# A two-layer decoder trunk: products with V followed at once by the next logits, forget-gate sums later in the order

## The chip, the cores and the metric

The kernel runs on one core of one Trainium2 chip. The metric is the device time of one execution in microseconds (us). Lower is better. Five engines matter: TensorE (PE in the rows, PEld its weight loads), VectorE (DVE), ScalarE (ACT), GpSimd (POOL) and SyncE (SP), which here only issues transfers.

## The reference, cut to what matters

x is 256 tokens by 1024 features, in float32. There are two layers, each a mixer of four groups of four heads (head width 64; 96 for MLA's queries and keys) and a SwiGLU. Layer 0 has two groups of forgetting attention (Fox) and two of stick-breaking attention, layer 1 has two of MoBA and two of MLA.

```python
for layer in range(2):
    h = rms_norm(x, norm[layer])
    x = x + mixer(h @ w_in) @ w_out          # 4 groups of 4 heads
    h = rms_norm(x, ffn_norm[layer])
    g, u = split(h @ w_gate_up, 2)
    x = x + (silu(g) * u) @ w_down           # 2816 wide

# Fox: q and k are normed for each head, f is one forget gate for each token and head
log_f = log_sigmoid(f + forget_bias)
c = cumsum(log_f, axis=tokens)
logits[t, s] = q[t] . k[s] / 8 + c[t] - c[s]     # s <= t
out = softmax(logits) @ v
```

## The kernel before

**Products.** Each large product is made of three matmuls in the fp32r format: operands are split into a rounded part and a rest (`whi` and `wlo` for weights, `xh` and `xl` for activations), and `mm3` adds three products. ScalarE makes `whi` from the loaded `raw`, VectorE makes `wlo` as the difference, in pieces of 128x512. Weights stream through four `raw` buffers and three pairs of split buffers. Pieces are split ahead of their use: `W.pos` is told how far TensorE is, and issues the splits due.

**Attention.** Logits, transposes and products with V are fp32 matmuls. A group's work is written as `prep` (norms' scaling has made `qkn` for queries and keys; four transposes each, and copies to `fT`), and then, for each of its two pairs of heads, `scores` (the logits into two PSUM banks, then the first step of the softmax or of the stick-breaking weights on VectorE), `transp` (three transposes a head, copied to `wt` by ScalarE) and `values` (products with V into the bank O, shared by the two pairs). After the second pair `outputs` copies O out. Logits, transposes, copies of `fT` and O share four PSUM banks, called `ps`.

**Order.** Between these steps `heads_loop` puts filler: the projections of the later groups and, at the end, three of the four parts of the output projection. A planner, `Flow`, writes the program's order. Its clock `clk` advances with each matmul that is issued, by an assumed cost (122 ns for 256 columns, 107 ns for a transpose). `fl.at(dt, fn)` puts a function due `dt` ns later, and it is called at the first stop of the filler at which the clock has passed the due time. `fl.pull(ns)` issues filler until its goal has grown by `ns`; a unit of filler is mostly one k-tile of a projection, six matmuls of 256 columns, 730 ns by the clock. `fl.need(flag)` issues filler until a flag is set.

The framework then places each engine's instructions, in an order fixed when the program is built: by priority, which is the place in the program, and by its own estimate of when operands are there. Functions marked `urgent` stand 400 places further ahead. On TensorE, functions marked `pinned` may not come before the last matmul issued ahead of them. `scores` is urgent and not pinned, so it may move ahead of filler that is written before it; `transp` and `values` are both urgent and pinned.

In `heads_loop` one iteration handles one pair of heads: the logits of pair i, then filler, the transposes of pair i-1, after every second pair the preparation of the next group, filler, the products of pair i-1, filler. Here `b` is the filler still planned, divided by the pairs still to come.

**The forget gates.** `first` is called before the projections of group 0's queries and keys. It puts these steps due: `chain` (the logs of the gates, `lf`), `gains`, `sums` (two transposes of `lf`, then the scan `cum` along the tokens on VectorE, and transfers of four rows of it to `cbc` for group 1 through DRAM), `columns` (two transposes of `cum`, copied to `ct` by VectorE) and `over(0)` and `over(1)` (four transposes each, which spread columns of `ct` over the partitions, copied to `cbc` by ScalarE). `masks` of group 0 reads `ct` and `cbc`: heads 0 and 1 what `over(0)` has written, heads 2 and 3 what `over(1)` has written. `masks(0)` and `masks(1)` are issued by `prep`, the other two after the first logits.

Of the kernel before, what the change touches and what calls it, by code (L numbers as in the profile page):

```python
# [281 lines left out]
def trunk_kernel(ctx: ExitStack, tc: tile.TileContext, x, ffn_norm, w_gate_up, w_down, rel_bias,  # L282
# [15 lines left out]
    fl = Flow()  # L298
# [12 lines left out]
    def pinned(fn):  # L311

        def f(*a, **k):
            with tc.issue_after(fl.last):
                return fn(*a, **k)
        return f
# [13 lines left out]
    def freed(*a):  # L330
        for t in a:
            read.add(id(t))

    def ps():
        return psB.tile([P, 512], F32, name=nm("ps"), tag="ps")
# [33 lines left out]
    def tr(o, i, idn):  # L369
        fl.last = pe.transpose(o, i, idn).ins  # L370
        fl.clk += 107
# [245 lines left out]
    def v_rows(V, src, scale):  # L617

        for tok in range(2):
            act.activation(V[:, tok], src[tok], AF.Identity, scale=1.0 if scale is None else scale[:, tok:tok + 1])  # L620
        return V
# [133 lines left out]

    def heads_loop(groups, lead):

        n, tail = 2 * len(groups), 6000
        fl.pull(lead)
        pinned(groups[0].prep)()  # L760
        fl.pull(100)
        for i in range(n + 1):
            b = max(fl.total - tail - fl.used, 0) / (n - i) if i < n else tail
            if i < n:
                if i > 0:
                    g.ready(pr, "e")
                g, pr = groups[i // 2], i % 2
                g.scores(pr)
            fl.pull((0.35 if i < n else 0.6) * b)
            if i > 0:  # L770
                g1, pr1 = groups[(i - 1) // 2], (i - 1) % 2
                g1.ready(pr1, "w")
                for j in range(2):
                    g1.transp(2 * pr1 + j)
            if i < n and pr == 1 and i + 1 < n:
                groups[i // 2 + 1].prep()
            fl.pull((0.35 if i < n else 0.15) * b)
            if i > 0:
                if g1.V is None:
                    fl.need(("V", g1))  # L780
                g1.values(pr1)
                if pr1 == 1:
                    g1.outputs()
            fl.pull((0.35 if i < n else 0.25) * b)


    xn = {}
# [208 lines left out]
    def first():  # L996

        zg, ng, ab, ex, lg, lf = (att.tile([P, 2, 8], F32, name=f"fg{i}", bufs=1) for i in range(6))

        @urgent  # L1000
        def chain():
            for tok in range(2):
                dve.scalar_tensor_tensor(zg[:, tok], fa[tok][:, 256:264], X.rs[:, tok:tok + 1], fb8,
                                         OP.mult, OP.add)
            dve.tensor_scalar(ng, zg, -1.0, 0.0, op0=OP.mult, op1=OP.max)
            dve.scalar_tensor_tensor(ab, ng, 2.0, zg, OP.mult, OP.add)
            act.activation(ex, ab, AF.Exp, scale=-1.0)
            act.activation(lg, ex, AF.Ln, bias=1.0)
            dve.tensor_tensor(lf, ng, lg, OP.add)
            groups[0].V = v_rows(vz[0], [t[:, :256].rearrange("p (h d) -> p h d", d=64) for t in fa], X.rs)  # L1010
            freed(*fa)
            fl.flags.add(("V", groups[0]))

        @pinned
        @urgent
        def sums():
            p_ = ps()
            for tok in range(2):
                tr(p_[:8, tok * P:tok * P + P], lf[:, tok], ident)
            dve.tensor_tensor_scan(cum, p_[:8, :256], mcaus[:8, P:P + 1].to_broadcast([8, 256]), 0.0, OP.add, OP.add)  # L1020
            pool.dma_start(cd, cum[4:8])
            pool.dma_start(cbc[:, 4:8], bass.AP(tensor=cd.tensor, offset=cd.offset, ap=[[0, P], [256, 4], [1, 256]]))

        @pinned
        @urgent
        def over(j):
            p_ = ps()
            for i in range(2):
                for tok in range(2):
                    c = tok * 8 + 2 * j + i  # L1030
                    tr(p_[:, i * 256 + tok * P:i * 256 + tok * P + P], ct[:, c:c + 1].to_broadcast([P, P]), ident)
            act.activation(cbc[:, 2 * j:2 * j + 2], p_.rearrange("p (i n) -> p i n", i=2), AF.Copy)

        @pinned
        @urgent
        def columns():
            p_ = ps()
            for tok in range(2):
                tr(p_[:, tok * 8:tok * 8 + 8], cum[:, tok * P:tok * P + P], ident[:8, :8])
            dve.tensor_copy(ct, p_[:, :16])  # L1040
        fl.at(1500, chain)
        fl.at(11800, sums)
        fl.at(13800, columns)
        fl.at(8000, gains)
        for j in range(2):
            fl.at(14300 + 1000 * j, lambda j=j: over(j))

    class Fox(Softmax):
        def mask(self, h):
# [75 lines left out]
    def fill_group(g):  # L1125
        G = groups[g]
        feat = g >= 2
        if g == 0:
            first()
            yield True  # L1130
        pq, pk = Proj(f"q{g}", X, feat), Proj(f"k{g}", X, feat)
        if feat:
            aq, ak = G.rows(pq, pk)
        else:
            aq, ak = G.normed(pq, pk, X.rs, r2, g_fox)
        yield from pq.kts(0, KT)
        if g == 0:
            dve.scalar_tensor_tensor(r2, X.rs[:, 0:2], 1.0 / 64, X.rs[:, 0:2], OP.mult, OP.mult)
        aq()
        yield from pk.kts(0, KT)  # L1140
        ak()
        if g == 0:
            X.row_bc()
            return
        pv = Proj(f"v{g}", X)
        yield from pv.kts(0, KT)
        G.V = urgent(v_rows)(vz[g % 2], heads_of(pv.a), X.rs)
        freed(pv.a)
        fl.flags.add(("V", G))
# [12 lines left out]
    run(fill_group(0))  # L1162
    fl.start(fill0(), 12 * 5235)
    heads_loop(groups, 2500)
    fl.drain()
    fl.finish()
# [249 lines left out]

    fl.start(fill1(), 6 * 5235 + 2 * 3300)
    heads_loop([moba[0], mla[0], moba[1], mla[1]], 2500)
    fl.drain()
    fl.finish()  # L1420
# [49 lines left out]
```

## Time and profile before

| | |
|---|---|
| time, median of 3 runs | 624.66 us (624.04 to 625.13) |
| time of the profiled execution | 625.75 us |
| its span, first to last instruction | 623.6 us |
| mean granted clock of TensorE | 0.997 |
| TensorE busy | 613.6 us |
| VectorE busy | 425.5 us |
| ScalarE busy | 336.2 us |
| attention of layer 0, by the trace | about 24 to 124 us |
| attention of layer 1, by the trace | about 338 to 432 us |

The span is one profiled execution of the program. The durations in the rows of the trace come from it. TensorE's matmuls are pipelined and the ends that the rows show are modelled, so the distance between starts tells more than the durations. The granted clock is a share of 2.4 GHz: 1.00 is full, 0.50 is 1.2 GHz, and a value between them is a mean over a stretch with both. Nearly every row has line 113 (L113), a helper through which all engines' instructions go, so instructions are told apart by their tiles.

### The profile page before, as it was taken

To read this page: it belongs to the slowest core of one execution; us is meant where nothing else is said; L and a number is where in the kernel's file an instruction comes from. 1 tells how busy PE (TensorE), PEld (TensorE's weight loads), DVE (VectorE), ACT (ScalarE), POOL (GpSimd) and SP (SyncE) were. 2 spreads that over 40 slices of the span, in tenths; PEclk is the share of its full clock that TensorE was granted. 3 is DMA by queue.
4 is the path that set the end of the run, shared out by engine and by line. 5 is a ranking of instruction groups with operands and counts; after the bars stand their busy time and mean duration, and the time that the engine had idled before them with its cause. 6 is when DMAs were issued, how large, how long until landed. Compare 5 with 4: busy or idle time off the path is not lost. (4 is left out here: it accounts for less than half of the span.)

```text
span 623.6 us, 11055 instructions
## 1 busy us (share of the span) xinstructions
PE 613.6 (98%) x4370; PEld 563.7 (90%) x4370; DVE 425.5 (68%) x915; ACT 336.2 (54%) x715; POOL 19.5 (3%) x50
## 2 busy tenths in 40 slices
PE   8989999999999999999999999999999999999997
PEld 7978898789999999988889988868999999998897
DVE  4889786576777677745547797977677767774541
ACT  6846675564444544545447676967544454453430
POOL 7200000010000000000000000000000000000000
PEclk9989999999999999999999999999999999999999
DMA  8963434447654754664558344154466465465500
GB/s 253 335 202 105 167 136 136 136 152 255 211 195 143 225 175 154 218 198 152 182 174 276 127 135 136 34 171 136 133 211 198 137 220 185 143 230 188 189 29 34
DMA packets 84213, 106.19 MB, mean 170 GB/s; under 512 B 3533, under 2 KB 69395, under 8 KB 84033
## 3 DMA queue, kind: packets, MB, share of 16 engines
q1 hardware_dynamic: 82880, 101.49, 50.5%
q0 software_dynamic: 1120, 3.86, 1.9%
q8 instruction: 34, 0.56, 0.4%
q14 instruction: 19, 0.15, 0.1%
q10 hardware_dynamic: 160, 0.14, 0.1%
HBM read 104.41 MB, written 3.17 MB: 173 GB/s over the span
## 5 line engine op out<-in xcount | busy, mean ns | idle before, releaser
L113 DVE TENSOR_TENSOR wlo<-raw,whi 128x512 fp32r<-128x512 f32 (+3 forms) x300 | 241.2, 828 | 84.3 <-ACT whi L113 83.7
L113 ACT ACTIVATE whi<-raw 128x512 fp32r<-128x512 f32 (+3 forms) x300 | 208.8, 739 | 142.6 <-PE acc L113 129.1
L113 PE MATMUL acc<-xh,whi 128*128 128x256 f32 x768 | 218.3, 284 | 0.0
L113 PE MATMUL acc<-xh,wlo 128*128 128x256 f32 x768 | 217.7, 284 | 0.0
L113 PE MATMUL acc<-xl,whi 128*128 128x256 f32 x768 | 217.5, 283 | 0.0
L113 PEld LDWEIGHTS acc<-xh,whi 128*128 128x128 f32 x768 | 147.3, 192 | 1.0 <-issue 1.0
L113 PEld LDWEIGHTS acc<-xh,wlo 128*128 128x128 f32 x768 | 147.3, 192 | 0.5 <-issue 0.5
L113 PEld LDWEIGHTS acc<-xl,whi 128*128 128x128 f32 x768 | 147.4, 192 | 0.0
L113 PE MATMUL acc<-whi,hl 128*128 128x512 f32 (+1 forms) x198 | 73.3, 370 | 0.0
L113 PE MATMUL acc<-whi,hh 128*128 128x512 f32 (+1 forms) x198 | 73.2, 370 | 0.0
L113 PE MATMUL acc<-wlo,hh 128*128 128x512 f32 (+1 forms) x198 | 73.1, 369 | 0.0
L113 PE MATMUL acc<-whi,xh 128*128 128x256 f32 (+2 forms) x240 | 71.1, 297 | 0.0
L113 PE MATMUL acc<-whi,xl 128*128 128x256 f32 (+2 forms) x240 | 70.0, 292 | 0.0
L113 PE MATMUL acc<-wlo,xh 128*128 128x256 f32 (+2 forms) x240 | 69.8, 291 | 0.0
L113 ACT ACTIVATE hh<-t 128x256 fp32r<-128x256 f32 x44 | 18.4, 418 | 69.6 <-DVE t L113 69.6
L113 DVE TENSOR_TENSOR gs<-acc,rbc 128x512 f32<-128x512 f32 x44 | 30.4, 691 | 37.0 <-PE acc L113 36.9
L113 PEld LDWEIGHTS acc<-whi,xh 128*128 128x128 f32 x240 | 46.0, 192 | 1.5 <-issue 1.3
L113 PEld LDWEIGHTS acc<-whi,xl 128*128 128x128 f32 x240 | 46.1, 192 | 0.7 <-issue 0.7
L113 PEld LDWEIGHTS acc<-wlo,xh 128*128 128x128 f32 x240 | 46.1, 192 | 0.6 <-issue 0.3
L113 PEld LDWEIGHTS acc<-whi,hh 128*128 128x128 f32 x198 | 37.3, 188 | 6.7
L113 PEld LDWEIGHTS acc<-whi,hl 128*128 128x128 f32 x198 | 37.2, 188 | 6.7
L113 PEld LDWEIGHTS acc<-wlo,hh 128*128 128x128 f32 x198 | 37.3, 188 | 6.7
(178 smaller groups left out, 626.5 us busy)
## 6 DMA issues: line engine op xcount, KB each, us to landing
raw<-in_ffn_w_gate_up SPq DMA_DIRECT2D x44, 1024.0 KB, 5.3
raw<-in_ffn_w_down SPq DMA_DIRECT2D x20, 1024.0 KB, 5.1
raw<-in_ev_w_in SPq DMA_DIRECT2D x10, 1024.0 KB, 8.0
raw<-in_od_w_in SPq DMA_DIRECT2D x6, 1024.0 KB, 5.5
raw<-in_ev_w_out SPq DMA_DIRECT2D x4, 1024.0 KB, 4.9
raw<-in_od_w_out SPq DMA_DIRECT2D x4, 1024.0 KB, 5.0
brep<-bd POOLq DMA_DIRECT2D x1, 2048.0 KB, 10.1
raw<-in_ffn_w_down SPq DMA_DIRECT2D x4, 512.0 KB, 3.7
```

The costliest lines, as they stand in the source:

```text
L113: r = f(*a, **k)
```

## The change

In `heads_loop` the third pull of an iteration is dropped, except in the last iteration, and the first two pulls grow from 0.35 to 0.5 of b. So in the program's order the products of pair i-1 are followed directly by the logits of pair i+1. In `first`, `columns` is due at 16,300 instead of 13,800, and `over(j)` at 16,800 + 1000 j instead of 14,300 + 1000 j. The matmuls, copies and transfers are the same.

```diff
-            fl.pull((0.35 if i < n else 0.6) * b)
+            fl.pull((0.5 if i < n else 0.6) * b)
             if i > 0:
                 g1, pr1 = groups[(i - 1) // 2], (i - 1) % 2
                 g1.ready(pr1, "w")
@@
             if i < n and pr == 1 and i + 1 < n:
                 groups[i // 2 + 1].prep()
-            fl.pull((0.35 if i < n else 0.15) * b)
+            fl.pull((0.5 if i < n else 0.15) * b)
             if i > 0:
                 if g1.V is None:
                     fl.need(("V", g1))
                 g1.values(pr1)
                 if pr1 == 1:
                     g1.outputs()
-            fl.pull((0.35 if i < n else 0.25) * b)
+            if i == n:
+                fl.pull(0.25 * b)
@@
         fl.at(1500, chain)
         fl.at(11800, sums)
-        fl.at(13800, columns)
+        fl.at(16300, columns)
         fl.at(8000, gains)
         for j in range(2):
-            fl.at(14300 + 1000 * j, lambda j=j: over(j))
+            fl.at(16800 + 1000 * j, lambda j=j: over(j))
```

## Rows read from the trace of the kernel before

**Rows 1.** The page, busy time: us, share of the span, instructions.

```profile
PE 613.6 (98%) x4370; PEld 563.7 (90%) x4370; DVE 425.5 (68%) x915; ACT 336.2 (54%) x715; POOL 19.5 (3%) x50
```

**Rows 2.** Waits of TensorE: us in total, times, longest.

```profile
PE ps L113 <- DVE sm L113: 2.2, 1, 2.2
PE ps L113 <- DMA x<-in_x: 1.1, 1, 1.1
```

**Rows 3.** Timeline of TensorE, 30.5 to 34 us: start, duration, [idle before].

```profile
30.97 0.28 PE L113 MATMUL acc<-whi,xh 128*128 128x256 f32 x1
31.09 0.28 PE L113 MATMUL acc<-wlo,xh 128*128 128x256 f32 x1
33.56 0.38 PE L113 MATMUL ps<-ident,cum 8*128 8x8 f32 x2 [2.19 <-DVE sm L113]
```

**Rows 4.** Timeline, 28 to 42 us: the gates' transposes, and VectorE.

```profile
28.25 0.38 PE L113 MATMUL ps<-ident,fg 128*8 128x128 f32 x2
...
32.83 0.67 DVE L113 TENSOR_TENSOR_SCAN cum<-ps,mcaus 8x256 f32<-8x256 f32 x1
...
34.16 0.17 DVE L113 COPY ct<-ps 128x16 f32<-128x16 f32 x1
...
35.05 0.69 DVE L113 TENSOR_TENSOR wlo<-raw,whi 128x512 fp32r<-128x512 f32 x1
37.33 1.41 DVE L113 SCALAR_TENSOR_TENSOR m<-cbc,ct,mcaus 128x128 f32<-128x128 f32 x4 [1.60 <-ACT cbc L113]
...
41.84 0.69 DVE L113 TENSOR_REDUCE sm<-sqh 128x8 f32<-128x512 f32 x1 [0.51 <-ACT sqh L113]
```

**Rows 5.** Stretches: length, busy us (instructions) by engine, granted clock, DMA share, GB/s.

```profile
31.00:34.00 3.00, 0.81 (x7) 0.59 (x5) 3.00 (x8) 0.68 (x3) 0.20 (x1) 0.89 1.06 303
34.00:37.00 3.00, 3.00 (x16) 3.00 (x16) 1.73 (x7) 0.43 (x2) 0.33 (x1) 0.54 0.76 242
37.00:40.00 3.00, 2.92 (x26) 2.75 (x25) 2.67 (x9) 1.50 (x3) 0.59 (x1) 1.00 0.99 314
```

**Rows 6.** Timeline, 36 to 39 us: copies to `cbc`, four transposes at full clock.

```profile
36.62 1.19 ACT L113 ACTIVATE cbc<-ps 128x512 f32<-128x512 f32 x2 [2.57 <-PE ps L113]
...
38.44 0.60 PE L113 MATMUL ps<-ident,qkn 128*128 128x128 f32 x4
```

**Rows 7.** Stretches of layer 0's attention.

```profile
41.50:57.30 15.80, 14.88 (x126) 13.96 (x124) 15.34 (x61) 13.08 (x39) 0.00 (x0) 1.00 0.06 16
57.30:112.00 54.70, 54.70 (x432) 47.80 (x432) 42.14 (x91) 33.57 (x80) 0.00 (x0) 1.00 0.46 154
```

**Rows 8.** Timeline, 41 to 60 us: first logits, group 1's key, products, logits.

```profile
41.57 1.58 PE L113 MATMUL ps<-fT,fT 64*128 64x128 f32 x16
...
55.99 0.68 DVE L113 TENSOR_TENSOR qkn<-acc,sm 128x512 f32<-128x512 f32 x1
...
56.73 0.66 PE L113 MATMUL ps<-ident,qkn 128*128 128x128 f32 x4 [0.92 <-DVE qkn L113]
...
58.11 0.39 PE L113 MATMUL acc<-xh,wlo 128*128 128x256 f32 x1
...
59.02 0.93 PE L113 MATMUL ps<-fT,fT 64*128 64x128 f32 x8
```

**Rows 9.** Timeline of TensorE, 63 to 83 us: logits (fT, sbT) and products (wt).

```profile
63.35 1.30 PE L113 MATMUL ps<-fT,fT 64*128 64x128 f32 x8
...
67.65 0.87 PE L113 MATMUL ps<-wt,V 128*64 128x256 f32 x8
...
74.33 0.87 PE L113 MATMUL ps<-wt,V 128*64 128x256 f32 x8
75.13 0.93 PE L113 MATMUL ps<-sbT,sbT 64*128 64x128 f32 x8
...
81.14 1.65 PE L113 MATMUL ps<-sbT,sbT 64*128 64x128 f32 x8
```

## The prediction

> **What bounds the kernel now.** I read the page first: TensorE is busy for 613.6 of 623.6 us, VectorE for 425.5 [rows 1]. So the span is TensorE's own work plus the little that it loses, and a change of order can win only what is lost: idle time, slow clock, and breaks between kinds of matmul. The list of waits, cut to TensorE, says where: one wait of 2.2 us on VectorE is the largest, every other is 1.1 us or less [rows 2]. The timeline puts it before the two transposes of `columns`: the matmul before them starts at 31.09, they start at 33.56 [rows 3]. They wait for `cum`, the scan of the forget gates' logs. Its input was transposed at 28.25, yet VectorE starts the scan at 32.83 and ends it at 33.50 [rows 4], because VectorE works in order and is full: in 31 to 34 us it is busy for 3.00 of 3.00 [rows 5], with splits of weights (`wlo`) between the steps of two chains. The stretches show a second price: the granted clock is 0.89 in 31 to 34 us, 0.54 in 34 to 37 and 1.00 after that [rows 5]. TensorE's clock has the levels 1.2 and 2.4 GHz, so these mean some 0.66 and 2.76 us at the lower one. In the first stretch TensorE idled through part of that (only from 33.56 on, 0.44 us, does it work), so the loss is (0.44 + 2.76)/2 = 1.6 us. Stall and clock are 2.19 + 1.6 = 3.8 us, the most that the place can give.
>
> **The change: the forget gates.** Nothing is added or removed, only due times move. By the planner's clock, `heads_loop` begins at 12,001 ns (2 x 8 k-tiles of 730 ns and three transposes of 107). `sums` fires after k-tile 1 of the next projection (at 12,731, to 12,945 with its transposes). k-tiles 2 and 3 end at 13,675 and 14,405: there `columns` fires now, due at 13,800. Due at 16,300 it fires after k-tile 6, at 16,595. Three more k-tiles, 18 matmuls at the 0.12 us of rows 3, go ahead of it: 2.16 us of work for a gap of 2.19. TensorE would come to the transposes at about 33.4, when the scan ends. The stall goes almost wholly, and as TensorE then works through, I take the drop of the clock to go too.
>
> What is late next is VectorE. `ct`, the copy behind `columns`, ran at 34.16 between two splits [rows 4]. Three k-tiles later in the order, the splits behind it, the last one at 35.05, may well stand ahead of it, for they are ready and VectorE's order is fixed. So it runs at 34.2 as now or at about 35.75, when the last of them ends. Behind it wait the four transposes of `over(0)`, which fire right after `columns` (16,809 against a due time of 16,800), the copy to `cbc` and the masks. With one k-tile of filler between, TensorE comes to `over(0)` at 34.6 and waits up to 1.3 us. Four transposes take 0.60 us with their drain, half a copy of `cbc` 0.60 [rows 6]; from `ct` at 35.75 to 35.92, with 0.1 for the hand-over, the masks start at 37.2. The other half, `over(1)`, falls behind the first logits; its heads' masks are needed only a pair later.
>
> VectorE is then the limit up to the preparation of group 1. Between 31 and 57.3 us it idles little beyond 1.60 (masks at 37.33, waiting for `cbc`) and 0.51 (a reduce at 41.84) [rows 4, 7]. The scaling of group 1's key, `qkn` at 55.99, stands at the end of that queue, and TensorE's transposes of it at 56.73 already wait 0.92 us for it [rows 8]. However early TensorE comes, it can't pass this point sooner than VectorE lets it. VectorE's gain has two ends. With `ct` late: the masks start 0.13 sooner, the scaling of group 0's key (0.68, as the one at 55.99) moves into the gap before them, and the 0.51 goes, since that reduce waits for a projection which TensorE ends sooner: 1.3 us. With `ct` as early as now, both idle times go: 2.1. I take the middle, 1.7. TensorE's own gain is 3.8 less about 0.7 of new waiting at `over(0)`; what exceeds 1.7, some 1.4, becomes more waiting at 56.73 (0.92 grows to about 2.3). From 57.3 to 112 us TensorE is busy all the time, with VectorE at 42.1 of 54.7 [rows 7], so what is won by then stays won. The ends for the whole place are 0 (all comes back as waiting and slow clock) and 3.8.
>
> The page "TensorE: Matmul & The Clock Gate" of the Trainium skill (its section on the 32x32 sub-arrays) says that ScalarE's and VectorE's queues are strictly first in, first out, and rows 4 agree: the scan waited 4 us behind other work with its input there. By it group 1's key can't overtake the splits and the sum for this place is 1.7; could each step run as soon as its input is there, it would be 3.8.
>
> **The change: the loop.** Dropping the third pull puts each pair's logits behind the products with V in program order, but `urgent` already lets them pass filler. Of the twelve places in both layers where a pair's products are followed by new logits, the logits stand at once behind the products in four (74.33 and 75.13 is one), ahead of the products, behind transposes, in six (63.35, with the products only at 67.65), and only in two is there filler between [rows 8, 9]. In one of these six matmuls fill 58.11 to 59.02, 0.91 us for 6 x 0.12 = 0.72 of work [rows 8]; the other, near 386, has two matmuls. Closing such a break gives back 0.2, so 0.4 for both. Filler that leaves this place goes between transposes and products (0.5 of b instead of 0.35), where the copy of `wt` has more time, which I count as nothing. The filler is the same work: 3 x 0.35 = 1.05 of b becomes 2 x 0.5, and the rest is drained behind. So 0.4, with the ends 0 and 0.4 x 12/2 = 2.4, if every place had such a break.
>
> **Sum.** 1.7 + 0.4 = 2.1 us. The profiled execution took 625.75, 2.15 around its span; with the change its span would be 621.5 and its time 623.65. It lies 1.09 above the median of the runs, 624.66, so I forecast 622.5. A change under 0.2%, 1.25 us, can't be told from none.
>
> **Rivals.**
> - *The whole 3.8 comes through.* VectorE's order is made anew; if the critical steps get ahead of splits, neither `ct` nor the group's key is late. For it: splits run far ahead of their use, so nothing needs them at once. Against it: the same priorities made the order that shows the lag. 3.8 + 0.4 = 4.2, 620.5.
> - *The stall moves and the clock falls again.* TensorE waits up to 1.3 at `over(0)` and 2.3 at group 1's key. In the trace 2.19 us idle was followed by the lower level, 0.92 was not [rows 3, 5, 7, 8]. Another 1.6 lost leaves 0.5: 624.1, the same as before. It decides from a single wait about as long as the old one; against it, the waiting may be spread over `over(0)`, the key of group 0 and both transposes of group 1.
> - *Slower: logits wait for PSUM banks.* With O held, two banks under transposes and no filler between, logits would wait for a bank. Those behind transposes show it: eight records take 1.30 us at 63.35 and 1.65 at 81.14, those behind products 0.93 [rows 9], so 0.37 and 0.72 more. If the other six places came to stand so, at 0.72 each, 4.3 is lost: 624.66 - 2.1 + 4.3 = 626.9. It decides from 0.56 a place, (2.1 + 1.25)/6. Against it: logits right behind products show no such wait now, as `wt` has left its banks by then.
> - *The loop's change does nothing.* The logits' places stay as they are; 1.7 alone, 623.0, still faster.
>
> **Chances.** Forecast, with the last rival: 0.55, own range 621.4 to 623.4. Whole gain: 0.15. Clock falls again, or VectorE keeps nearly all: 0.2. Slower: 0.1. Faster by over 0.2% takes the first two and loses a little at the edge: 0.67; within 0.22; slower 0.11. The range runs from the whole gain, a little below it, 620.2, to a little above the repeated drop, 624.8; it leaves out the slower case and the tails.
>
> **What would show it.** Right: no wait before the transposes of `cum`, granted clock 1.00 over 31 to 37 us; `ct` between 34 and 36; first logits at 39 to 40 instead of 41.57; a longer wait before group 1's key, now near 55; logits in the loops at their old places. Wrong: group 1's key transposed at 53 (whole gain); a second stretch at the lower level in 36 to 58; or logits in the loops that take over 1.3 us each.

## The result

The change made the kernel slower: median 633.63 us (632.83 to 633.89, 4 runs) against 624.89 (624.04 to 625.7, 4 runs), a ratio of 1.0138 [1.012, 1.0155]. The forecast was 622.5 (620.2 to 624.8). The profiled execution took 632.83 us, its span 630.7 at a granted clock of 0.999. The busy line of its page answers [rows 1]:

```profile
PE 622.2 (99%) x4370; PEld 565.5 (90%) x4370; DVE 426.3 (68%) x915; ACT 336.9 (53%) x715; POOL 20.2 (3%) x50
```

As many matmuls as before, yet TensorE is busy for 8.6 us longer, while VectorE and ScalarE are busy as long as before (within 0.8 us). TensorE doesn't wait more for others; its own work takes longer. Its waits (us in total, times, longest), beside [rows 2]:

```profile
PE ps L113 <- DVE sm L113: 1.7, 1, 1.7
...
PE ps L113 <- DVE qkn L113: 0.6, 1, 0.6
PE ps L113 <- DVE ct L113: 0.4, 1, 0.4
```

The stretches (length, busy us and instructions of TensorE, its weight loads, VectorE, ScalarE and GpSimd, granted clock, DMA share, GB/s) say where it happens; they answer [rows 5, 7]:

```profile
31.00:34.00 3.00, 1.28 (x10) 0.91 (x8) 3.00 (x9) 0.42 (x2) 0.53 (x1) 1.00 1.02 289
34.00:37.00 3.00, 2.64 (x22) 2.44 (x22) 2.93 (x11) 1.21 (x3) 0.00 (x0) 1.00 0.73 202
...
41.50:57.30 15.80, 15.24 (x119) 13.56 (x117) 15.01 (x55) 9.90 (x28) 0.00 (x0) 1.00 0.11 28
57.30:112.00 54.70, 54.70 (x400) 46.15 (x399) 37.79 (x83) 31.56 (x75) 0.00 (x0) 1.00 0.43 147
```

At the gates the place is better: clock 1.00, more matmuls by 37 us. From 57.3 to 112 us TensorE is busy all the time, as before, but issues 400 matmuls instead of 432. That is where the loss shows, and a busy share can't show it. TensorE's timeline at such a place (start, duration, shape, count; an fp32 matmul leaves two records, so x2 is one matmul):

```profile
75.20 0.65 PE L113 MATMUL ps<-wt,V 128*64 128x256 f32 x2
75.78 0.48 PE L113 MATMUL ps<-sbT,sbT 64*128 64x128 f32 x2
76.19 0.65 PE L113 MATMUL ps<-wt,V 128*64 128x256 f32 x2
76.77 0.70 PE L113 MATMUL ps<-sbT,sbT 64*128 64x128 f32 x4
77.40 0.43 PE L113 MATMUL ps<-wt,V 128*64 128x128 f32 x2
77.77 0.70 PE L113 MATMUL ps<-sbT,sbT 64*128 64x256 f32 x2
78.39 0.43 PE L113 MATMUL ps<-wt,V 128*64 128x128 f32 x2
78.75 0.38 PE L113 MATMUL acc<-whi,xh 128*128 128x256 f32 x1
```

The four products of a pair (V below) and the four logits of the next (S) are no longer two blocks, VVVVSSSS as at 74.33 and 75.13 of [rows 9], but alternate: VSVSSVSV. From 75.20 to 78.75 they take 3.55 us; as blocks the products took 0.80 (74.33 to 75.13) and the logits 0.85, so 1.65 (the filler behind them starts at 75.98). The place costs 1.90 us more. The trace has four of them (54.80, 75.20, 100.60 and 389.45) and a fifth, VSVSVSVS, in the MLA heads (413.32 to 417.20, 3.88 us against some 2.2 as blocks): 4 x 1.90 + 1.7 = 9.3 us. A part of why an alternating place is dear is seen in its weight loads, which elsewhere overlap the matmuls (in brackets, the idle time ahead of them):

```profile
75.78 0.29 PEld L113 LDWEIGHTS ps<-sbT,sbT 64*128 64x128 f32 x2 [0.38 <-issue]
76.19 0.19 PEld L113 LDWEIGHTS ps<-wt,V 128*64 128x64 f32 x2
76.77 0.30 PEld L113 LDWEIGHTS ps<-sbT,sbT 64*128 64x128 f32 x4 [0.39 <-issue]
77.40 0.19 PEld L113 LDWEIGHTS ps<-wt,V 128*64 128x64 f32 x2 [0.33 <-issue]
77.76 0.29 PEld L113 LDWEIGHTS ps<-sbT,sbT 64*128 64x128 f32 x2 [0.17 <-issue]
78.39 0.19 PEld L113 LDWEIGHTS ps<-wt,V 128*64 128x64 f32 x2 [0.33 <-issue]
...
78.86 0.19 PEld L113 LDWEIGHTS acc<-wlo,xh 128*128 128x128 f32 x1
```

At each of the six turns between weights of 128 rows x 64 columns and weights of 64 rows x 128 columns the load comes late: it starts together with its own matmul (75.78, 76.19, 76.77, 77.40, 77.76, 78.39), where the filler's load at 78.86 runs ahead of its matmul at 78.98. The idle time ahead of it is 0.33 to 0.39 us at four of the turns, 0.17 at one, and too short to be listed at 76.19. Over the span this line of the list of waits grows from 14 times, 3.3 us, to:

```profile
PEld ps L113 <- issue: 10.7, 38, 0.4
```

### The profile page after: what moved, and what is told of

Its sections match the earlier page's. It is cut to its first block, busy times and chain, and to the rows that moved or that the text cites. A ratio compares the mean times of both kernels' runs of the same rounds, so it can differ in the third digit from the quotient of the medians.

```text
span 630.7 us, 11055 instructions
## 1 busy us (share of the span) xinstructions
PE 622.2 (99%) x4370; PEld 565.5 (90%) x4370; DVE 426.3 (68%) x915; ACT 336.9 (53%) x715; POOL 20.2 (3%) x50
## 4 chain that ended last, share of the span: by engine, by line
PE 89%; DVE 4%; DMA 3%; ACT 2%; issue 1%; SPq 1%; DVEq 0%; ACTq 0%; POOLq 0%
PE acc L113 79%; PE ps L113 10%; DMA raw<-in_ev_w_in 1%; DVE wlo L113 1%; DVE sm L113 1%; ACT whi L113 1%; DMA x<-in_x 1%; DMA cbc<-cd 1%; DMA cd<-cum 1%; ACT pm L113 1%; DVE m L113 0%; SPq L430 0%; DVE qkn L113 0%; DVE pm L113 0%; DVE lg L113 0%
```

## The experiments

Medians are beside the kernel before on the same chip: 625.1 (19 runs) for the first four, 625.01 (14) for the next four, 624.77 (12) for the last three. The "aligned" difference is worked out from the traces: the start of the same filler matmul in two executions, compared in the last FFN (the SwiGLU), less the difference that they had at 30.7 us, ahead of the gates, from the first loads. For the change it is +8.0 us against the profiled execution of before. Theory: alternation is the loss. Rivals: the gates; logits that wait for banks (the forecast's slower case); the new pulls putting transposes and products at worse places; the data's type, or the break of the filler, rather than the shapes.

**One half each.** e1_loop_alone has the new pulls and the old due times (edits are shown cut, `...`, and against the kernel after where nothing else is said):

```diff
-        fl.at(16300, columns)
+        fl.at(13800, columns)
...
-            fl.at(16800 + 1000 * j, lambda j=j: over(j))
+            fl.at(14300 + 1000 * j, lambda j=j: over(j))
```

> The loop's new pulls with the old due times. Theory (alternation): TensorE's order now alternates single products with V and single logits of the next pair at three places (V S V S S V S V) and once in MLA (V S V S V S V S), where the kernel before runs four products and then four logits. In the trace of the changed kernel such a place takes 3.55 us against 0.80 + 0.85 = 1.65, and the MLA one 3.88 against about 2.2: 3 x 1.9 + 1.7 = 7.4 us, so 631.5 to 633. Rival 1 (the late sums cost the time): no more than 1 us from the kernel before, 624 to 626. Rival 2 (logits wait for PSUM banks at all places): also slow, but with idle time before logits instead of alternation.

Measured: 631.33 (630.96 to 632.69, 4 runs, as for every median without a count), 1.0117 [1.0098, 1.0136], aligned +6.1. Its trace has VSVSSVSV at two places of layer 0 and one of layer 1, and the MLA place. e2_gates_alone has the three pulls of before and the new due times:

```diff
-            fl.pull((0.5 if i < n else 0.6) * b)
+            fl.pull((0.35 if i < n else 0.6) * b)
...
-            if i == n:
-                fl.pull(0.25 * b)
+            fl.pull((0.35 if i < n else 0.25) * b)
```

> The late due times with the old loop. Theory (alternation): TensorE's order has no alternating place beyond the one of before, so this is faster by what the place of the stall gives back, 1 to 2 us: 622.9 to 623.9. Rival 1 (the late sums cost the time, because they stand in front of the first logits and upset the order behind): slower by several us, 628 or more.

Measured: 623.39 (622.92 to 624.28, 10 runs), 0.998 [0.997, 0.9991], aligned -1.55. So the gates' step gains 1.7 by the medians, and the whole loss is the loop's: its order has no new alternating place.

**The same program without alternation.** e3_pinned_logits is the whole change, with the logits held behind the last matmul written ahead of them; e4_pinned_layer0 holds those of layer 0 alone:

```diff
+        @pinned
         @urgent
         def scores(self, pr):
```

> The whole change, but logits may not come before the last product issued ahead of them, so that each place runs four products and then four logits. Theory (alternation): all that was lost comes back, 622.5 to 624.5. Rival 2 (no filler between products and logits, so logits wait for PSUM banks): it stays above 630, since still no filler stands between them. Rival 3 (the new pulls put transposes and products at worse places): above 628.

> As the one before, but logits are held back in layer 0 alone; layer 1 keeps its two alternating places. Theory (alternation): 1.9 + 1.7 = 3.6 us above the kernel with both layers held back, about 626.5 to 628, half-way to the changed kernel. Rivals 2 and 3: no step of that size that belongs to the two places.

e3: 620.5 (620.01 to 621.3), 0.9943 [0.9924, 0.9963], aligned -5.6: all of the loss comes back, and 2 us more than the theory expected. Wherever products and logits stand together they are VVVVSSSS, but for one SVSVVVSS in the MLA heads, which the kernel before has too. TensorE's timeline there, the place that stood at 75.20:

```profile
72.90 0.87 PE L113 MATMUL ps<-wt,V 128*64 128x256 f32 x8
73.70 0.93 PE L113 MATMUL ps<-sbT,sbT 64*128 64x128 f32 x8
74.55 0.38 PE L113 MATMUL acc<-whi,xh 128*128 128x256 f32 x1
```

1.65 us again, with nothing waiting, though the logits stand right behind the products: no waiting for banks. e4: 625.11 (624.49 to 628.37, 10 runs), 1.001 [0.9997, 1.0024], 4.6 above e3 where 3.6 was expected; of the 13.1 us between the change and e3, 8.5 come from layer 0 and 4.6 from layer 1. Of the 13.1, 9.3 are the alternating places. For the rest no run was made. A part can be read from the trace of after: logits that stand right behind transposes take longer, 1.23 us for eight records at 62.06 and again at 106.42, against 0.85 behind products, and at 82.47 the two heads' logits come apart, each head's taking 0.85 by itself (82.47 to 83.32, 83.64 to 84.49):

```profile
82.47 0.92 PE L113 MATMUL ps<-sbT,sbT 64*128 64x128 f32 x4
83.32 0.39 PE L113 MATMUL acc<-xh,whi 128*128 128x256 f32 x1
83.64 0.92 PE L113 MATMUL ps<-sbT,sbT 64*128 64x128 f32 x4
```

That is 0.38 + 0.85 + 0.38 = 1.6 us in layer 0, where e3 has no logits right behind transposes. What is left, some 2 us, is open.

**Is it the turns?** Three kernels hold each product and each logits matmul behind the last one. Two of them write products and logits as one chain in all twelve places: e5_pairs_kept as VVSSVVSS, e6_alternate as VSVSSVSV. e7_head_by_head keeps the blocks, but within each block one head's two matmuls go before the other's, in the logits too:

```diff
+PATTERN = "VVSSVVSS"
...
+        for c in pattern:
+            with tc.issue_after(fl.last):
+                (V if c == "V" else S).pop(0)()
...
```

```diff
-            for b in range(2):
-                for i in range(2):
+            for i in range(2):
+                for b in range(2):
...
```

> The kernel with the whole change and logits held back (620.5 us), but in all twelve places the order is forced to V V S S V V S S: three changes between products and logits instead of one, the two heads of a pair still next to each other. Theory P (what alternation costs is mostly that the two heads of a pair no longer run side by side on the two halves of the array): each place about 0.1 to 0.3 us more than the 1.65 of four and four, 621.5 to 624. Rival S (each change between the two kinds costs, 1.9 us over the six further changes of an alternating place, 0.32 each): two more changes at twelve places, 0.63 x 12 = 7.6 us more, 628.

> The same kernel with V S V S S V S V forced in all twelve places, the order that the changed kernel has in four. Both P and S expect 1.9 us at the eight places with logits of 64-row heads and somewhat less, some 1.3 to 1.7, at the four of MLA: 15.2 + 6 = 21, so 638 to 643. If the alternation is only a mark of another cause, well below that, under 630.

> The kernel with the whole change and logits held back, products and logits still in blocks of four, but in each block both matmuls of the first head and then both of the second. No change between products and logits is added. Theory P: of a block's 0.64 us of streaming only the second matmul of the first head and the first of the second can run side by side, so a block of products takes about 1.1 instead of 0.8: some 0.3 to 0.45 us for each of 16 blocks of products and 12 of logits, 8 to 12 us more, 629 to 633. Rival S: no cost, 620 to 622.

e5: 626.67 (626.01 to 627.65, 10 runs), 1.0026 [1.0016, 1.0035], between what the two theories expected and in the range of neither. e6: 641.1 (640.91 to 641.23), 1.0249 [1.0234, 1.0265], so (641.1 - 620.5)/12 = 1.72 a place over e3, near the 1.90 read from the rows: forced in twelve places, alternation costs in twelve. e7: 620.64 (620.47 to 620.94), 0.9921 [0.9905, 0.9938], the same as e3 within the noise. That refuted a part of the theory: two heads' matmuls need not be neighbours in the order to run side by side, and the 8 to 12 us that it expected did not come. A place of e7:

```profile
73.41 0.88 PE L113 MATMUL ps<-wt,V 128*64 128x256 f32 x8
74.22 0.93 PE L113 MATMUL ps<-sbT,sbT 64*128 64x128 f32 x8
```

The products take 0.81 us, as in e3, and within the first row the second head's first matmul starts 0.01 us behind the first head's, though both of the first head's stand ahead of it in the program. So it is enough that a block is of one shape; within it neither half of the array waits for the other. A place of e5:

```profile
74.12 0.65 PE L114 MATMUL ps<-wt,V 128*64 128x256 f32 x4
74.70 0.49 PE L114 MATMUL ps<-sbT,sbT 64*128 64x128 f32 x4
75.12 0.44 PE L114 MATMUL ps<-wt,V 128*64 128x128 f32 x4
75.49 0.70 PE L114 MATMUL ps<-sbT,sbT 64*128 64x256 f32 x4
76.12 0.39 PE L114 MATMUL acc<-whi,xh 128*128 128x256 f32 x1
```

Two matmuls of the two heads take 0.58, 0.42, 0.37 and 0.63 us here; one alone takes 0.58, 0.41, 0.37 and 0.62 in the place of after. A lone one leaves half of the array idle for just as long. So the price of an alternating place has two parts, by an estimate from these rows. The first is the columns that stream through the array: 128 columns more cost 0.21 us (0.58 against 0.37; at 2.4 GHz that is 4 cycles a column), so the streams alone are 0.43 us for 256 columns and 0.21 for 128. A place has four of each, 2.56 us. In blocks all run two side by side, 1.28; alternating, only the two middle logits do, 2.35. So 1.07 is lost. The second is the turns, six instead of one: (1.90 - 1.07)/5 = 0.17 us each. A turn from transposes shows the same price: six transposes in front of logits take 0.75 us (81.72 to 82.47 in the trace of after), in front of filler 0.57 (97.70 to 98.27). By that e5, with two more turns and no lost side, costs 0.34 a place; its row gives 2.00 against 1.65, but its median is 6.2 us above e3's, 0.51 a place, and what the other 0.16 is was not traced.

**Filler between the products.** e9_spread puts filler behind each of a pair's first three products:

```diff
+                    if b + i < 2:
+                        with tc.issue_after(fl.last):
+                            fl.unit()
```

> The kernel with the whole change and logits held back (620.5 us), but between the four products of each pair stands a unit of filler: full 128x128 matmuls, six of 256 columns or three of 512. It asks whether any break into single products costs, or only the turn between products (weights of 64 columns) and logits (64 rows). Some 45 single products more stand beside filler on both sides. If every change of weight shape costs what a turn between products and logits does (0.26 to 0.29 us), two more changes for each of 45: 23 us more, 643. If only the end of a block costs what the closed breaks gave back, 0.2 each: 9 us, 629. If filler beside a product costs nothing: 620 to 622.

Its filler ran ahead of plan, so that some products probably read a later group's V (two buffers of V serve all groups; this is read from the program, not traced). It is no longer the same computation, but its instructions are as many (4370 of TensorE). Measured: 652.41 (652.03 to 654.16), 1.0449 [1.0429, 1.0468], 31.9 us above e3, more than any theory expected.

```profile
55.17 0.65 PE L113 MATMUL ps<-wt,V 128*64 128x256 f32 x2
55.74 0.39 PE L113 MATMUL acc<-xh,whi 128*128 128x256 f32 x1
...
56.65 0.65 PE L113 MATMUL ps<-wt,V 128*64 128x256 f32 x2
...
58.13 0.43 PE L113 MATMUL ps<-wt,V 128*64 128x128 f32 x2
...
59.40 0.43 PE L113 MATMUL ps<-wt,V 128*64 128x128 f32 x2
59.77 0.49 PE L113 MATMUL ps<-fT,fT 64*128 64x128 f32 x4
```

The place takes 4.60 us; less 18 filler matmuls at 0.12 (2.16) that is 2.44 for products that take 0.80 in a block: four alone (0.57 + 0.57 + 0.36 + 0.37 = 1.87), and each run of six filler matmuls takes 0.91 instead of 0.72 (55.74 to 56.65). That is 1.64 more for a pair, for 16 pairs 26 of the 31.9 us; the rest was not traced. Filler between products costs them as much as logits do: not the kind of work, but the break of a block counts. It isn't the data's type either: in the trace of after, six transposes in fp32 of full 128x128 weights alternate with three filler matmuls between 71.58 and 72.52, 0.94 us, what they take apart (6 x 0.095, as at 97.70, + 3 x 0.12).

**What each half is worth without alternation.** e8_oldloop_pinned is e2 with the logits pinned, e10_newloop_pinned_early is e3 with the old due times. e11_behind adds to e3 that logits and transposes also stand behind the last product:

```diff
+        @pinned
+        @behind
         @urgent
         def scores(self, pr):
...
+                    lastv.append(fl.last)
```

> Late due times and logits held back, but with the old loop's three pulls, so that filler stands between products and logits at nine or ten places. It tells what the change's idea is worth by itself, closing that break. By the breaks in the trace of the kernel before, 0.2 us each: about 2 us above the 620.5 of the same kernel with the new loop, 622 to 623. If the breaks cost nothing, 620 to 621, and then holding the logits back is the whole gain.

> The new loop with logits held back, but the old due times of the forget gates. It tells what the late gates are worth where nothing alternates: by the trace 1 to 2 us, so 621.5 to 622.5 against 620.5. If the late gates give nothing beyond what happens to be won with the old order: 620 to 621.

> The whole change with logits held back, and logits and transposes also held behind the last product issued, so that the two places in layer 1 where products still stand among logits or transposes are closed too. Each is about 0.8 us in the trace of the kernel without it (3.07 against 2.2 us): 619 to 620, the fastest yet. If these two places are hidden by other waits near the end of layer 1: 620.5.

e8: 623.08 (622.75 to 623.79, 5 runs), 0.9965 [0.9952, 0.9978]: pinning alone gains 0.3 over e2, which isn't clear of noise, and the new pulls another 2.6 (e3; 3.2 aligned). e10: 621.51 (621.04 to 621.7), 0.9947 [0.9931, 0.9964]: the late due times are worth 1.0 there, and that is mostly the clock, which fell in all four runs of e10 (mean 0.997; the two runs of e3 with such a mean take 620.92 and 621.3). The stretch of its trace beside [rows 5]:

```profile
34.00:37.00 3.00, 3.00 (x16) 3.00 (x15) 2.11 (x7) 1.19 (x2) 0.00 (x0) 0.50 0.70 193
```

e11: 621.34 (620.88 to 623.6, 7 runs), 0.9953 [0.9937, 0.9969]: nothing over e3, a miss. The fastest are e3 and e7, which can't be told apart, 0.6% and 0.8% faster than before by their ratios.

## Why the prediction was wrong

**What bounds the kernel** stood: TensorE does. But "a change of order can win only what is lost" has another side that was not asked: an order can also lose what the old one had, two heads side by side.

**The gates** were right in size: 1.7 forecast, 1.7 by e2's median, 1.55 aligned. That is partly luck. The 1.7 was made up of idle times of VectorE, while most of what e2 gains is the clock: where the mean clock was 1.0 in both, before took 623.6 to 624.2 us (6 runs) and e2 622.9 to 623.6 (5 runs), only some 0.6 apart. The way there was otherwise, too. Not 18 more matmuls went ahead of `columns` but 7, 30 behind the transposes of `fg` instead of 23, where the planner's count for the kernel before is 12: the framework had already let later filler pass it. So the stall fell only from 2.19 to 1.72 us instead of going. The gates' timelines of after, and the stall in e3, beside [rows 3, 4, 8]:

```profile
30.98 0.28 PE L113 MATMUL acc<-whi,xl 128*128 128x256 f32 x1
32.98 0.29 PE L113 MATMUL ps<-ident,cum 8*128 8x8 f32 x2 [1.72 <-DVE sm L113]
```

```profile
32.80 0.29 PE L113 MATMUL ps<-ident,cum 8*128 8x8 f32 x2 [0.37 <-DVE sm L113]
```

```profile
32.26 0.67 DVE L113 TENSOR_TENSOR_SCAN cum<-ps,mcaus 8x256 f32<-8x256 f32 x1
...
34.20 0.17 DVE L113 COPY ct<-ps 128x16 f32<-128x16 f32 x1
35.96 1.40 DVE L113 SCALAR_TENSOR_TENSOR m<-cbc,ct,mcaus 128x128 f32<-128x128 f32 x4
...
52.41 0.68 DVE L113 TENSOR_TENSOR qkn<-acc,sm 128x512 f32<-128x512 f32 x1
```

How long the stall is depends on how early TensorE comes, too, and that differs between executions: with the same due times it is 1.18 us in e2 and 0.37 in e3, where the last filler starts at 31.40 and 32.15 instead of 30.98 and the scan ends at 32.8 in both. On VectorE the scan is 0.57 us sooner than before, `ct` at the early of the two times forecast (34.2), the masks at 35.96 instead of 37.33. The due times alone didn't do this: e1, which has the old ones and no drop of the clock, has the scan at 32.07, `ct` at 33.40 and the masks at 35.29. Group 1's key is scaled 3.58 us sooner, at 52.41, and TensorE waits 0.56 us for it instead of 0.92, so the longer wait there did not come; the new wait for `ct` ahead of `over(0)` is 0.4, where 0.7 was forecast. That it is sooner by nearly the whole 3.8 doesn't mean 3.8 won, since less filler stands ahead of it (307 matmuls instead of 318); aligned at the same filler, e2 wins 1.55.

**The clock** stayed up in the profiled execution, as forecast, and in two of the other three runs. But it is a smaller term than taken, since only some executions of before have the drop: of its 19 runs beside e1 to e4, the 6 with a mean clock of 1.0 take 623.6 to 624.2 us, the 13 with 0.994 to 0.997 take 624.2 to 626.5. The profiled one was of the second kind. Nor does the stall alone decide: in e10 the clock fell to 0.50 after 1.59 us of waiting for the scan, in e1 it stayed at 1.00 after 1.91.

**The loop** is the step that failed. It asked only whether filler stands between products and logits, found that in two places, took the logits to stay "at their old places", and gave 0.4. Two things were not seen. With no filler between, products and logits are neighbours of equal urgency, the products pinned and the logits not, and the order came out alternating in five places. And alternation has a price, 1.90 us a place, for which the sum had no term; the bounds from 0 to 2.4 were all on the side of a gain. The trace of before could have shown it. One of the six places that the prediction counted as logits ahead of the products alternates there already, in the MLA heads, as SVSVVVSS, and takes 2.99 us, against 2.22 for the two blocks ahead of it:

```profile
408.50 0.87 PE L113 MATMUL ps<-wt,V 128*64 128x256 f32 x8
...
410.72 0.82 PE L113 MATMUL ps<-ident,pm 128*128 128x128 f32 x6
411.62 0.49 PE L113 MATMUL ps<-mT,mT 96*128 96x128 f32 x2
412.04 0.65 PE L113 MATMUL ps<-wt,V 128*64 128x256 f32 x2
412.61 0.49 PE L113 MATMUL ps<-mT,mT 96*128 96x128 f32 x2
413.03 0.86 PE L113 MATMUL ps<-wt,V 128*64 128x256 f32 x6
413.83 1.13 PE L113 MATMUL ps<-mT,mT 96*128 96x256 f32 x4
414.61 0.58 PE L113 MATMUL acc<-whi,oh 128*128 128x512 f32 x1
```

That the framework alternates them because consecutive products write the same bank, so that it takes a ready logits matmul between two of them, is argued from the order, not shown. With the logits held in place, the same change of the loop gains 2.6 us (e8 to e3), just above the upper bound.

**The rivals.** The slower one had the right sign and the wrong mechanism: logits right behind products show no wait for a bank in e3, and the 626.9 it gave is 6.7 short. The whole gain and the clock falling again did not come. That the loop's change does nothing was wrong by some 10 us (e2 to after).

Beside this: the page "TensorEngine Tiling (Array Packing)" of the Trainium skill, section Key Properties, says that changing the tiling mode, and not just the tile, drains TensorE; the late weight loads at the turns agree, with 0.33 to 0.39 us idle ahead of four of the six in a place. The page "TensorE: Matmul & The Clock Gate", Part 3 (packing small matmuls), says that matmuls in different tiles run concurrently; the pairs that take no longer than one alone agree (0.58 us).

## What to carry to other kernels

Where small matmuls use halves of the array, count the turns between shapes in TensorE's order, not only its idle time: here a turn cost some 0.17 us and a matmul without its neighbour as much as two, and a busy share of 99% showed neither. When two urgent groups become neighbours in program order, fix their order as blocks, or the scheduler may interleave them; the same change with one group pinned went from 1.4% slower to 0.6% faster. And read the order of the instructions that a program has before counting the filler that a due time moves: the framework may already have moved it.

## What was not expected of the hardware

A half-array fp32 matmul alone takes what two in both halves take (0.58 us with 256 columns, 0.37 with 128). Within a block of one shape the order of the two halves' matmuls makes no difference (e7, 620.64 us against 620.5). Full-array filler between half-array products is no cheaper than logits there: a run of six takes 0.91 instead of 0.72 us. Full-array fp32 transposes between filler matmuls cost nothing extra (0.94 us for six and three, against 0.93 apart). The clock fell in only some executions of one program, after waits of 2.19 us (before) and 1.59 (e10), and not after one of 1.91 (e1).
